# Up projections of a conv-gated MLP: two couples of groups per layer with tokens on the partitions, parking in later groups

## The chip, the cores and the metric

The kernel runs on one core of a Trainium2 chip, as one launch. The metric is the device time in microseconds, the median over the runs, with the lowest and highest of them. Besides, one execution was recorded by the hardware profiler; its rows are what "the trace" means here. All times are microseconds unless marked otherwise.

## The reference

A trunk of two layers works on x of 256 tokens by 2048, all in fp32. Each layer mixes tokens (layer 0 a spatial gating unit, layer 1 a latent attention), adds the residual, normalizes, and then runs a gated MLP with a causal convolution of width 3:

```python
def conv_ffn(x, w_up, conv_w, conv_b, w_down):
    h = x @ w_up                       # 256 x 2048 by 2048 x 11008
    h = lax.conv_general_dilated(h, conv_w[:, None, :], ...) + conv_b
    a, g = jnp.split(h, 2, axis=-1)
    return (jax.nn.silu(g) * a) @ w_down

x = layer_norm(ALPHA * x + m, ln_mix_g[i], ln_mix_b[i])
f = conv_ffn(x, ffn_w_up[i], ffn_conv_w[i], ffn_conv_b[i], ffn_w_down[i])
x = layer_norm(ALPHA * x + f, ln_ffn_g[i], ln_ffn_b[i])
```

The change concerns `h = x @ w_up` of both layers.

## The kernel before, in words

**Numbers in two parts.** TensorE multiplies fp32r parts. Every fp32 weight is split into a high part, a cast on ScalarE (`_cast`, L127), and a low part, the rest, a subtraction on VectorE (L130); activations are split likewise (`xhl`: 256 columns high and 256 low). A product takes high by high, high by low and low by high.

**The feed.** `Feed` holds one list of weight chunks of 1 MB (128 x 2048) in the order of use. `next()` gives the next chunk's parts and keeps loads (SP's queue, `_load`) and splits (`_split`) some chunks ahead. The parts lie in slots of the "big" pool, so a split waits until TensorE is through with the chunk that held its slot before. A chunk has a kind. A plain one ("") is split in two halves of 1024 columns. A "wide" one is split whole. A "seven" one (`_seven`) holds a 2 x 2 arrangement of four 512-column blocks; besides high and low parts of three blocks, VectorE builds sums of blocks (`ts`, L137) which are split as well (`th`, `tl`), so that seven block products do the work of eight. The other factor has to be summed in the same way (`xs`, split into high and low in `combine`).

**Two ways round.** In `prod_a` the weights stand still and the tokens move: four accumulators per group, each a 128-feature block by 512 columns (tokens by the high part, tokens by the low part); a plain chunk takes 16 matmuls of 512 columns (high weights by both parts) and 16 of 256 (low weights by the high part). `sum_halves` adds the two halves when the group is done (a copy of the low half on ScalarE, L388, and an add on VectorE into `h`, L390). In `prod_b` the activations stand still and 512 columns of weights move; tokens lie on the partitions, and a wide chunk takes 24 matmuls of 512 columns, a seven chunk 21. The V and U stages, at the kernel's begin, and the down projections run that way, with the class `Banks`: `eight` for wide chunks, `seven` for seven chunks, `rest` for the four VectorE additions that make the results out of the seven products. Four accumulators (`DIRECT`: q3, p2, e, q4) take the direct sums and four (`OWN`: p1, q5, p7, p6) the own products: all eight PSUM banks.

**The up projection.** Per layer 86 plain chunks: group 0 is done at the boundary to the norm (`upf`), groups 1 to 20 have four chunks each and group 21 has two. A group gives two pairs (a block of `a` and the fitting block of `g`). `pair` runs each through the convolution (`conv`: a ScalarE step L994, two VectorE steps L995 and L997, twice), SiLU (L1011) and the product into `act` (L1012). The eight banks hold two groups, so a group's pairs are worked off while the next group's matmuls run.

**Beside it.** The down projection will use eight chunks per layer whose seven-sums are prepared ahead during the up projection, "parked": `park` loads a chunk on GpSimd's queue (`praw`), splits and sums it (L154, L168, L169) and stores the parts to DRAM; `fetch` brings them back later. It is cut into steps, and each `next(jobs)` in the group loop does one: load, first split and store, sums, second split and store. Before, two steps stand in each group from 2 on (the second and third chunk), until the eight chunks are through. Also in this loop the norm's residual is multiplied and shifted (`old.restore`, groups 2 to 5) and put away in DRAM (`old.park`, groups 4 and 6).

The order of the instructions on each engine is set by a scheduler from the program's order and dependencies, except for the parts pinned into program order (parking, and some of TensorE's).

Of the kernel before, what the change touches and what calls it, by code (L numbers as in the profile page):

```python
# [8 lines left out]
F32 = mybir.dt.float32  # L9
F32R = mybir.dt.float32r  # L10
# [58 lines left out]
FIRST = ((19, 1), (20, 0), (20, 2))  # L69
LEAD = 5  # L70
KEEP = {"wide": 4, "seven": 6, "parked": 6}


def plan(n_k):
# [137 lines left out]
def trunk(ctx: ExitStack, tc: tile.TileContext, x, xT, gm_in, gm_wout, ffn_up, ffn_dn,  # L212
# [12 lines left out]
    def slot(shape, name, dt=F32, tag="big"):  # L225
        return big.tile(shape, dt, tag=tag, name=name, bufs=SLOTS[tag])
# [30 lines left out]
    def back(w, n_k):  # L257

        for hf, units in enumerate(plan(n_k)):
            c = slice(hf * 1024, (hf + 1) * 1024)  # L260
            for u, kind in units:
                if 2 * u + 1 == n_k:
                    chunks.append((w[2 * u, :, c], 1024, kind))
                    continue
                if kind == "parked":
                    parked.append(len(chunks))
                chunks.append((w[2 * u : 2 * u + 2, :, c].rearrange("k p c -> p k c"), 2048, kind))

    back(gm_wout, NF_GM)
    chunks += [(ffn_up[0, i], 2048, "") for i in range(n_up)]  # L270
    back(ffn_dn[0], NF_FF)
    chunks += [(ml_q[i], 2048, "") for i in range(4)]
    chunks += [(ml_kv[i], 3 * KVR, "") for i in range(5)] + [(ml_kv[5, :, 0:KVR], KVR, "")]
    chunks += [(ml_b[i], 2048, "") for i in range(ml_b.shape[0])]
    chunks += [(ml_out[i], 2048, "seven" if i - ml_out.shape[0] // 2 in MO_SEVEN else "") for i in range(ml_out.shape[0])]
    chunks += [(ffn_up[1, i], 2048, "") for i in range(n_up)]
    back(ffn_dn[1], NF_FF)


# [18 lines left out]
    def combine(name, o, k1, k2):  # L298


        t = tp.tile([P, 4, P], F32, tag="t2", name=f"xs{name}", bufs=T2)
        turn(t, k1, k2)
        o = o.rearrange("p (h s c) -> p h s c", h=2, s=4)
        nc.scalar.copy(o[:, 0], t)
        nc.vector.tensor_tensor(o[:, 1], t, o[:, 0].bitcast(F32), ALU.subtract)
        return [(o[:, 0, i], o[:, 1, i]) for i in (1, 2, 0, 3)]
# [221 lines left out]
    def down(n_k, src, tag, ln, acts, skew=SKEW, tiles=None, beside=None):  # L528

        ln.begin()  # L530
        seq = plan(n_k)
        line = seq[0] + seq[1]
        late, at = [], 0
        fetched = max([i for i, t in enumerate(line) if t[1] == "parked"], default=len(line))

        def again(v2, p):

            if src is not pT or p >= len(seq[0]) or v2 in line[p + 1 : p + 1 + KEEP[v2[1]]]:
                return None
            kind2 = dict(seq[1])[v2[0]]  # L540
            return "wide" if kind2 != v2[1] else kind2

        for hf, units in enumerate(seq):
            n = len(units)
            last = [u for u, kind in units if kind != "wide"][-1]
            acc = nxt if hf else Banks(f"{tag}{hf}", DIRECT + OWN, tiles)
            for i, (u, kind) in enumerate(units):
                left = n - 1 - i if hf == 1 else n
                if src is pT and at >= n - 3:
                    for v2 in line[at + 3 : at + 5]:  # L550
                        acts.bring(*v2)
                for n2, v2 in enumerate(line[at : at + 3]):
                    acts.make(*v2, again=again(v2, at + n2), tag="side" if at + n2 > fetched or at + n2 >= len(seq[0]) and v2[1] == "parked" and v2[0] < 20 else "big")
                if i == n - 8 and hf == 0:
                    ln.fetch(0)
                if i == n - 6 and hf == 0:
                    ln.fetch(1, "big" if src is pT else "side")
                if i == n - 2 and hf == 0:
                    nxt = Banks(f"{tag}1", OWN + DIRECT, seeded=True)
                    ln.seed(1, nxt)  # L560
                got = feed.next(splits=2 if left > 5 or left == 0 else 3, loads=2 if left > 2 or left == 0 else 1)
                if left == 6:
                    ln.prep()
                if left == 2 and ln.last:
                    ln.halves()
                if beside and at == 2:
                    beside()
                a, sums = acts.got[u]
                if left < skew:
                    late.append((a, *got))  # L570
                elif kind == "wide":
                    acc.eight(a, *got)
                else:
                    acc.seven(a, sums, *got, 512 if kind == "parked" else 0)
                    if u == last and hf:
                        parts = acc.rest(ln.room(hf))
                        if ln.last:
                            ln.whole(1, 3, acc.acc["q4"], parts[3])
                    elif u == last:
                        for j, t in enumerate(acc.rest()):  # L580
                            ln.fold(j // 2, 2 * hf + j % 2, t)
                at += 1
                for v2 in [v2 for v2 in acts.got if not any(v2 == w2 and n2 < KEEP[kind2]
                                                            for n2, (w2, kind2) in enumerate(line[at:]))]:
                    acts.got.pop(v2)
            if hf == 0:
                for j, m in enumerate(DIRECT):
                    ln.piece(j // 2, j % 2, acc.acc[m])

        def end(b, f):  # L590
            for i, (a, hi, lo) in enumerate(late):
                for j in range(len(a[b])):
                    prod_b([acc.acc[DIRECT[2 * b + f - 2]]], a[b][j], hi, lo, [(j * 1024 + (f - 2) * 512, 512)],
                           False, i == len(late) - 1 and j == len(a[b]) - 1)

        return [[None, None] + [acc.acc[DIRECT[2 * b + f]] for f in range(2)] for b in range(2)], end
# [404 lines left out]
    def ffn(layer, ln, acc, end, last):  # L1001
        act = [None] * 6
        acts = Acts(act, f"dn{layer}", NF_FF)

        def pair(a, acc_a, acc_g):
            if act[a // 8] is None:
                act[a // 8] = slot([P, 8, S], f"act{layer}_{a // 8}", tag="side" if a // 8 > 3 else "big")
            ca = conv(layer, a, acc_a, f"{layer}a{a}")
            cg = conv(layer, NF_FF + a, acc_g, f"{layer}g{a}")
            s = tp.tile([P, S], F32, tag="t1", name=f"s{layer}_{a}", bufs=T1)  # L1010
            nc.scalar.activation(s, cg, AF.Silu)  # L1011
            nc.vector.tensor_tensor(act[a // 8][:, a % 8, :], s, ca, ALU.mult)  # L1012

        hb, ht = [], [None, None]

        def after(b, step, acc):
            if step == 0:
                ht[b] = tp.tile([P, 512], F32, tag="t2", name=f"upt{layer}_{b}", bufs=T2)
                nc.scalar.copy(ht[b], acc)
                return  # L1020
            if b == 0:
                hb.extend(bank(f"uph{layer}_{f}") for f in range(2))
            for f in range(4):
                o = (f % 2) * S + b * P
                nc.tensor.transpose(hb[f // 2][:, o : o + P], ht[b][:, f * P : (f + 1) * P], ident)

        boundary(ln, acc, end, f"upf{layer}_", after)
        xhl, old = ln.new, ln
        jobs = park_all(feed.used + 2 * n_up)
        for gi in range(1, 22):  # L1030
            nt, nk = (4, 4) if gi < 21 else (2, 8)
            acc = [bank(f"up{layer}_{gi}_{f}") for f in range(nt)]
            for c in range(KD // nk):
                hi, lo = feed.next()
                prod_a(acc, xhl, range(nk * c, nk * c + nk), hi, lo)
                if gi > 1 and c in (1, 2) and gi + c > 3:
                    next(jobs, None)
                if (gi, c) in FIRST:
                    acts.make(*plan(NF_FF)[0][FIRST.index((gi, c))])
                if gi == 1 and c == 0:  # L1040
                    after(1, 1, None)
                    for f in range(2):
                        pair(f, hb[0][:, f * S : (f + 1) * S], hb[1][:, f * S : (f + 1) * S])
            for f in range(nt // 2):
                pair(2 * gi + f, acc[f], acc[nt // 2 + f])
            if 1 < gi < 6:
                old.restore(gi - 2)
            if gi in (4, 6):
                old.park(gi // 2 - 2)
        ln = Norm(2 * layer + 1, {}, old.put_away, last)  # L1050
        return (ln, *down(NF_FF, act, f"dn{layer}", ln, acts, 4 if last else SKEW))

# [429 lines left out]
```

## Time and profile before

| | |
|---|---|
| median of 3 runs | 2457.16 (2456.21 to 2458.2) |
| the profiled execution | 2456.78 |
| its span in the trace | 2454.6 |
| granted TensorE clock | 1.00 |
| GpSimd (POOL) busy | 140.3 |
| HBM read, written | 552.35 MB, 72.93 MB |

The page of the profile gives the busy time of each engine, the chain of work that ended last, the costliest groups of instructions and the transfers. A row of the timeline has start, duration, engine, line of the kernel, operation, what it writes and reads, shape and count. Durations of neighbours on one engine overlap; what an instruction costs in a queue is the distance from its start to the next start. PE is TensorE's matmuls, PEld its weight loads, DVE VectorE, ACT ScalarE, POOL GpSimd, SP SyncE.

### The profile page before, as it was taken

To read this page: it belongs to the slowest core of one execution; us is meant where nothing else is said; L and a number is where in the kernel's file an instruction comes from. 1 tells how busy PE (TensorE), PEld (TensorE's weight loads), DVE (VectorE), ACT (ScalarE), POOL (GpSimd) and SP (SyncE) were. 2 spreads that over 40 slices of the span, in tenths; PEclk is the share of its full clock that TensorE was granted. 3 is DMA by queue.
4 is the path that set the end of the run, shared out by engine and by line. 5 is a ranking of instruction groups with operands and counts; after the bars stand their busy time and mean duration, and the time that the engine had idled before them with its cause. 6 is when DMAs were issued, how large, how long until landed. Compare 5 with 4: busy or idle time off the path is not lost.

```text
span 2454.6 us, 32596 instructions
## 1 busy us (share of the span) xinstructions
PE 2447.1 (100%) x12394; PEld 2081.1 (85%) x12394; DVE 2099.4 (86%) x2813; ACT 1491.8 (61%) x2015; POOL 140.3 (6%) x261
## 2 busy tenths in 40 slices
PE   9999999999999999999999999999999999999999
PEld 7888888888888888888888888988888888888887
DVE  7999999889998788787779897878788787878998
ACT  6666665566576566556555566665665665656554
POOL 0000000001010000000000000000000000000000
PEclk9999999999999999999999999999999999999999
DMA  7555666659797778778868885544578787867895
GB/s 292 203 206 206 230 202 205 206 175 305 251 297 253 248 281 331 271 291 296 329 215 321 318 297 170 189 146 145 211 263 314 274 312 294 300 265 265 314 340 193
DMA packets 124668, 627.40 MB, mean 256 GB/s; under 512 B 11592, under 2 KB 15184, under 8 KB 83424
## 3 DMA queue, kind: packets, MB, share of 16 engines
q1 hardware_dynamic: 90128, 462.47, 53.2%
q0 software_dynamic: 34384, 162.86, 17.8%
q8 instruction: 97, 1.59, 0.3%
q14 instruction: 59, 0.48, 0.1%
HBM read 552.35 MB, written 72.93 MB: 255 GB/s over the span
## 4 chain that ended last, share of the span: by engine, by line
PE 97%; DVE 1%; DMA 1%; ACT 0%; issue 0%; SPq 0%; ACTq 0%; DVEq 0%
PE up L232 37%; PE ub L232 16%; PE dn_q L232 8%; PE dn_p L232 6%; PE v_q L232 5%; PE v_p L232 4%; PE wo_q L232 2%; PE dn_e L232 2%; PE wo_p L232 2%; PE upf L232 2%; PE mo L232 2%; PE v_e L232 2%; PE mkv L232 1%; PE qn L232 1%; PE mq L232 1%; PE kn L232 1%
## 5 line engine op out<-in xcount | busy, mean ns | idle before, releaser
L130 DVE TENSOR_TENSOR wl<-raw,wh 128x1024 fp32r<-128x1024 f32 (+4 forms) x643 | 950.9, 1493 | 145.0 <-ACT wh L127 112.9
L127 ACT CAST wh<-raw 128x1024 fp32r<-128x1024 f32 (+4 forms) x643 | 803.9, 1272 | 339.3 <-PE up L232 85.6
L232 PE MATMUL up<-xhl,wh 128*128 128x512 f32 x2624 | 611.3, 390 | 0.0
L232 PEld LDWEIGHTS up<-xhl,wh 128*128 128x128 f32 x2624 | 487.3, 188 | 97.8
L232 PEld LDWEIGHTS up<-xhl,wl 128*128 128x128 f32 x2624 | 325.8, 192 | 6.4
L232 PE MATMUL up<-xhl,wl 128*128 128x256 f32 x2624 | 328.1, 283 | 0.0
L127 ACT CAST th<-ts 128x1536 fp32r<-128x1536 f32 (+1 forms) x162 | 168.0, 1051 | 138.6 <-DVE ts L137 119.3
L130 DVE TENSOR_TENSOR tl<-ts,th 128x1536 fp32r<-128x1536 f32 (+1 forms) x162 | 191.1, 1217 | 6.4 <-PE v_p L232 1.9
L232 PE MATMUL ub<-wh,xhl 128*128 128x512 f32 x564 | 175.7, 393 | 0.0
L232 PEld LDWEIGHTS ub<-wh,xhl 128*128 128x128 f32 x564 | 105.9, 188 | 23.7 <-issue 1.9
L137 DVE TENSOR_TENSOR ts<-ts,raw 128x512 f32<-128x512 f32 x162 | 111.0, 685 | 1.6
L232 PE MATMUL ub<-wl,xhl 128*128 128x512 f32 x282 | 109.8, 389 | 0.0
L137 DVE TENSOR_TENSOR ts<-raw 128x1024 f32<-128x1024 f32 x81 | 98.6, 1217 | 2.3 <-DMA raw<-in_gm_in_dram 1.0
L232 PE MATMUL v_q<-wh,xhl 128*128 128x512 f32 x224 | 70.7, 391 | 0.8 <-ACT wh L127 0.8
L232 PEld LDWEIGHTS ub<-wl,xhl 128*128 128x128 f32 x282 | 52.9, 188 | 11.1
L232 PE MATMUL v_p<-wh,xhl 128*128 128x512 f32 x192 | 60.0, 389 | 0.0
L232 PEld LDWEIGHTS v_q<-wh,xhl 128*128 128x128 f32 x224 | 42.0, 188 | 10.3 <-ACT wh L127 1.6
L811 ACT ACTIVATE lny<-lnt,lncol 128x128 f32<-128x128 f32 x96 | 36.7, 472 | 15.3 <-PE lnt L807 15.2
L154 DVE TENSOR_TENSOR praw<-praw 128x512 f32<-128x512 f32 x64 | 43.9, 685 | 0.6
L390 DVE TENSOR_TENSOR h_1a<-up,lo_1a 128x256 f32<-128x256 f32 x41 | 17.2, 419 | 31.2 <-ACT lo_1a L388 31.2
L390 DVE TENSOR_TENSOR h_0a<-up,lo_0a 128x256 f32<-128x256 f32 x41 | 17.2, 419 | 31.0 <-ACT lo_0a L388 31.0
L232 PE MATMUL v_q<-wl,xhl 128*128 128x512 f32 x112 | 43.6, 389 | 0.0
(1992 smaller groups left out, 4442.1 us busy)
## 6 DMA issues: line engine op xcount, KB each, us to landing
raw<-in_ffn_up_dram SPq DMA_DIRECT2D x172, 1024.0 KB, 7.2
raw<-in_gm_in_dram SPq DMA_DIRECT2D x93, 1024.0 KB, 5.2
raw<-in_ffn_dn_dram SPq DMA_DIRECT2D x68, 1024.0 KB, 6.9
raw<-in_gm_wout_dram SPq DMA_DIRECT2D x48, 1024.0 KB, 6.6
praw<-in_ffn_dn_dram POOLq DMA_DIRECT2D x16, 1024.0 KB, 15.2
keptth<-pth POOLq DMA_DIRECT2D x16, 1024.0 KB, 8.8
kepttl<-ptl POOLq DMA_DIRECT2D x16, 1024.0 KB, 9.5
fth<-keptth POOLq DMA_DIRECT2D x16, 1024.0 KB, 10.4
```

What stands on the lines that cost most here:

```text
L127: cast = self.nc.scalar.copy(hi, raw)
L130: self.nc.vector.tensor_tensor(lo, raw, hi.bitcast(F32), ALU.subtract)
L137: add = lambda o, a, b: self.nc.vector.tensor_tensor(o, a, b, ALU.add)
L154: add = lambda o, a, b: pin(nc.vector.tensor_tensor(o, a, b, ALU.add))
L232: recent[0] = nc.tensor.matmul(o, l, r, start=start, stop=stop, skip_group_check=True)
L390: nc.vector.tensor_tensor(h, acc[:, 0:S], lo, ALU.add)
L811: nc.scalar.activation(y[:, j], t[:, j * P : (j + 1) * P], AF.Identity, bias=lncol[:, o : o + 1], scale=lncol[:, g : g + 1])
```

## The change

In each layer groups 5 and 6, and groups 8 and 9, become couples. A couple's eight chunks are cut anew: each takes one half (1024 columns) of the chunk of the same place in either group, so that it holds two steps of 128 along the 2048 inputs by the 512 features of each group, a 2 x 2 arrangement of blocks. They run with tokens on the partitions (`prod_b`, `Banks`, all eight banks) in the order `UP_PAIRS`; four of the eight are seven chunks. The activation sums for these are made in groups 2 to 4 by `combine_up`, four per layer. When the couple is done, `rest` and four adds give four tiles of 128 tokens by 512 features. After the first chunk of the plain group that follows, 16 transposes (`turn_back`) bring them back to features on the partitions, into four banks, and their four pairs are done after that group's second and third chunk, with no `sum_halves`.

Restoring and putting away the residual go to groups 1 to 4 (`EARLY`). Parking goes to one step each in groups 4 and 7 and three steps per group from group 10 on. The act tiles 0 and 1 now lie in the "side" pool and 2 to 5 in "big" (before: 0 to 3 in big, 4 and 5 in side).

```diff
+UP = [(1,), (2,), (3,), (4,), (5, 6), (7,), (8, 9), *((i,) for i in range(10, 22))]
+UP_PAIRS = [0, 2, 1, 3, 5, 4, 6, 7]
+UP_SEVEN = (2, 3, 4, 6)
+EARLY = {(1, 2): ("restore", 0), (2, 1): ("combine", 0), (2, 2): ("restore", 1), (2, 3): ("park", 0),
+         (3, 1): ("restore", 2), (3, 2): ("combine", 1), (3, 3): ("restore", 3), (4, 0): ("park", 1),
+         (4, 1): ("combine", 2), (4, 2): ("combine", 3)}
...
+    def up(w):
+        for gis in ((0,), *UP):
+            if len(gis) == 1:
+                chunks.extend((w[i], 2048, "") for i in range(4 * gis[0], min(4 * gis[0] + 4, n_up)))
+                continue
+            for p in UP_PAIRS:
+                i = 4 * gis[0] + p // 2
+                t = w[i : i + 5 : 4, :, p % 2 * 1024 : p % 2 * 1024 + 1024].rearrange("f p c -> p f c")
+                chunks.append((t, 2048, "seven" if p in UP_SEVEN else "wide"))
...
-                act[a // 8] = slot([P, 8, S], f"act{layer}_{a // 8}", tag="side" if a // 8 > 3 else "big")
+                act[a // 8] = slot([P, 8, S], f"act{layer}_{a // 8}", tag="side" if a // 8 < 2 else "big")
...
+        def turn_back(t, src, b):
+            for f in range(4):
+                o = (f % 2) * S + b * P
+                nc.tensor.transpose(t[f // 2][:, o : o + P], src[:, f * P : (f + 1) * P], ident)
+
+        def both(gi, t):
+            for f in range(2):
+                pair(2 * gi + f, t[0][:, f * S : (f + 1) * S], t[1][:, f * S : (f + 1) * S])
...
+        def combine_up(p):
+            x = xhl[p // 2][:, p % 2 * 2 : p % 2 * 2 + 2]
+            y = tp.tile([P, 2, S], F32, tag="t2", name=f"upy{layer}_{p}", bufs=T2)
+            nc.vector.tensor_tensor(y, x[:, :, 0:S].bitcast(F32), x[:, :, S : 2 * S].bitcast(F32), ALU.add)
+            if len(sums) % 2 == 0:
+                rooms.append(slot([P, 2, 8 * P], f"xu{layer}_{p}", F32R))
+            sums[p] = combine(f"u{layer}_{p}", rooms[-1][:, len(sums) % 2, :], y[:, 0], y[:, 1])
...
-                if gi > 1 and c in (1, 2) and gi + c > 3:
+                if c == 0 and turned:
+                    for i, t in enumerate(turned[2]):
+                        turn_back(turned[1][i % 2], t, i // 2)
+                if turned and 0 < c < 3:
+                    both(turned[0][c - 1], turned[1][c - 1])
+                if (gi > 9 and c > 0) or (gi, c) in ((4, 3), (7, 3)):
                     next(jobs, None)
...
+        def summed(gis):
+            acc = Banks(f"up{layer}_{gis[0]}", DIRECT + OWN)
+            for p in UP_PAIRS:
+                a = [[x_parts(xhl, 2 * p + j, b) for j in range(2)] for b in range(2)]
+                got = feed.next()
+                if p in UP_SEVEN:
+                    acc.seven(a, sums[p], *got, turned=512, across=True)
+                    if p == UP_SEVEN[-1]:
+                        rest = acc.rest()
+                else:
+                    acc.eight(a, *got, across=True)
+            for n, t in zip(DIRECT, rest):
+                nc.vector.tensor_tensor(t, acc.acc[n], t, ALU.add)
+            return gis, [[bank(f"upr{layer}_{gi}_{f}") for f in range(2)] for gi in gis], rest
```

How the order moves is shown at the start of the first couple, where group 4's four accumulators (`up0_4_0` to `up0_4_3`) are still to be read. On TensorE before, group 5's first chunk, chunk 164, begins with the weights (`wh164`) at rest and the activations moving:

```order
L232 MATMUL up0_5_0_7051<-xhl1_0_5891,wh164_6920 128x512 [waits Activation_49]
L232 MATMUL up0_5_1_7052<-xhl1_0_5891,wh164_6920 128x512 [waits DVE_49]
L232 MATMUL up0_5_2_7053<-xhl1_0_5891,wh164_6920 128x512 [waits DVE_49]
L232 MATMUL up0_5_3_7054<-xhl1_0_5891,wh164_6920 128x512 [waits DVE_49,PE_49]
L232 MATMUL up0_5_0_7051<-xhl1_0_5891,wh164_6920 128x512
```

On TensorE now, the couple's second and third chunks (165, a seven chunk, and 166, a wide one; `q5`, `q3`, `p2`, `p7` are accumulators of the couple, and an own product such as `p7` takes a bank that group 4 has to leave):

```order
L239 MATMUL up0_5_q5_7088<-th165_6997,xu0_2_6488 128x512 [waits DVE_49]
L239 MATMUL up0_5_q5_7088<-th165_6997,xu0_2_6488 128x512
L239 MATMUL up0_5_q5_7088<-tl165_6998,xu0_2_6488 128x512
L239 MATMUL up0_5_q3_7083<-wh166_7091,xhl1_0_5891 128x512 x2
L239 MATMUL up0_5_q3_7083<-wl166_7092,xhl1_0_5891 128x512
L239 MATMUL up0_5_q3_7083<-wh166_7091,xhl1_0_5891 128x512 x2
L239 MATMUL up0_5_q3_7083<-wl166_7092,xhl1_0_5891 128x512
L239 MATMUL up0_5_p2_7084<-wh166_7091,xhl1_0_5891 128x512 x2
L239 MATMUL up0_5_p2_7084<-wl166_7092,xhl1_0_5891 128x512
L239 MATMUL up0_5_p2_7084<-wh166_7091,xhl1_0_5891 128x512
L239 MATMUL up0_5_p7_7089<-th165_6997,xu0_2_6488 128x512 [waits DVE_49]
L239 MATMUL up0_5_p7_7089<-th165_6997,xu0_2_6488 128x512
```

What moved: the scheduler has put ten matmuls of chunk 166 between `q5` and `p7` of chunk 165; `p6` follows after three more matmuls of 166. `q5` takes the bank of `up0_4_2`, `p7` that of `up0_4_1` and `p6` that of `up0_4_3`, which VectorE reads for `h_0g8`, `h_0a9` and `h_0g9`.

On VectorE before, the same pairs of group 4 (8 and 9) stand between plain splits:

```order
L390 TENSOR_TENSOR h_0a8_7005<-up0_4_0_6828,lo_0a8_7003 128x256 [waits Activation_49]
L995 SCALAR_TENSOR_TENSOR c_0a8_7007<-h_0a8_7005,cst_176,c_0a8_7007 128x255 [waits Activation_49]
L390 TENSOR_TENSOR h_0g8_7013<-up0_4_2_6830,lo_0g8_7011 128x256 [waits Activation_49]
L997 SCALAR_TENSOR_TENSOR c_0a8_7007<-h_0a8_7005,cst_176,c_0a8_7007 128x254 [waits DVE_49]
L995 SCALAR_TENSOR_TENSOR c_0g8_7015<-h_0g8_7013,cst_176,c_0g8_7015 128x255 [waits Activation_49]
L997 SCALAR_TENSOR_TENSOR c_0g8_7015<-h_0g8_7013,cst_176,c_0g8_7015 128x254 [waits DVE_49]
L1012 TENSOR_TENSOR act0_1_7002<-s0_8_7019,c_0a8_7007 128x256 [waits Activation_49]
L390 TENSOR_TENSOR h_0a9_7024<-up0_4_1_6829,lo_0a9_7022 128x256 [waits Activation_49]
```

On VectorE now, between `h_0g8` and `h_0a9`:

```order
L408 TENSOR_TENSOR h_0g8_7055<-up0_4_2_6853,lo_0g8_7053 128x256 [waits Activation_49]
L1015 SCALAR_TENSOR_TENSOR c_0a8_7049<-h_0a8_7047,cst_176,c_0a8_7049 128x254 [waits DVE_49]
L144 TENSOR_TENSOR ts167_7121<-raw167_7008 128x1024 [waits DMAHW2_49,PE_49]
L1013 SCALAR_TENSOR_TENSOR c_0g8_7057<-h_0g8_7055,cst_176,c_0g8_7057 128x255 [waits Activation_49]
L144 TENSOR_TENSOR ts167_7121<-ts167_7121,raw167_7008 128x512 [waits DVE_49]
L1015 SCALAR_TENSOR_TENSOR c_0g8_7057<-h_0g8_7055,cst_176,c_0g8_7057 128x254 [waits DVE_49]
L137 TENSOR_TENSOR wl167_7123<-raw167_7008,wh167_7122 128x1536 [waits PE_49,Activation_49]
L144 TENSOR_TENSOR ts167_7121<-ts167_7121,raw167_7008 128x512 [waits DVE_49]
L1030 TENSOR_TENSOR act0_1_7044<-s0_8_7061,c_0a8_7049 128x256 [waits Activation_49]
L408 TENSOR_TENSOR h_0a9_7066<-up0_4_1_6852,lo_0a9_7064 128x256 [waits Activation_49]
```

What moved: the seven chunk 167's sums and first split now stand ahead of `h_0a9`, and the first of them waits (`PE_49`) until TensorE has left a slot. Lines of the changed kernel lie a little further down: L239, L137, L144, L408, L1013, L1015 and L1030 are L232, L130, L137, L390, L995, L997 and L1012 of before.

More of the change, by code (lines that the diff above doesn't have):

```diff
@@ L267, in back @@
                 chunks.append((w[2 * u : 2 * u + 2, :, c].rearrange("k p c -> p k c"), 2048, kind))
+    def up(w):
[7 more added lines that the diff above has]
+                chunks.append((t, 2048, "seven" if p in UP_SEVEN else "wide"))
     back(gm_wout, NF_GM)
-    chunks += [(ffn_up[0, i], 2048, "") for i in range(n_up)]
+    up(ffn_up[0])
     back(ffn_dn[0], NF_FF)
@@ L275, in trunk @@
     chunks += [(ml_out[i], 2048, "seven" if i - ml_out.shape[0] // 2 in MO_SEVEN else "") for i in range(ml_out.shape[0])]
-    chunks += [(ffn_up[1, i], 2048, "") for i in range(n_up)]
+    up(ffn_up[1])
     back(ffn_dn[1], NF_FF)
@@ L552, in down @@
                 for n2, v2 in enumerate(line[at : at + 3]):
-                    acts.make(*v2, again=again(v2, at + n2), tag="side" if at + n2 > fetched or at + n2 >= len(seq[0]) and v2[1] == "parked" and v2[0] < 20 else "big")
+                    acts.make(*v2, again=again(v2, at + n2), tag="side" if at + n2 > fetched else "big")
                 if i == n - 8 and hf == 0:
@@ L1022, in after @@
                 hb.extend(bank(f"uph{layer}_{f}") for f in range(2))
-            for f in range(4):
-                o = (f % 2) * S + b * P
-                nc.tensor.transpose(hb[f // 2][:, o : o + P], ht[b][:, f * P : (f + 1) * P], ident)
+            turn_back(hb, ht[b], b)
         boundary(ln, acc, end, f"upf{layer}_", after)
@@ L1029, in ffn, with plain @@
         jobs = park_all(feed.used + 2 * n_up)
-        for gi in range(1, 22):
+        sums, rooms = {}, []
+        def combine_up(p):
[5 more added lines that the diff above has]
+            sums[p] = combine(f"u{layer}_{p}", rooms[-1][:, len(sums) % 2, :], y[:, 0], y[:, 1])
+        early = {"restore": old.restore, "park": old.park, "combine": lambda i: combine_up(UP_SEVEN[i])}
+        def plain(gi, turned):
             nt, nk = (4, 4) if gi < 21 else (2, 8)
@@ L1041, in ffn @@
                     after(1, 1, None)
-                    for f in range(2):
-                        pair(f, hb[0][:, f * S : (f + 1) * S], hb[1][:, f * S : (f + 1) * S])
+                    both(0, hb)
+                if (gi, c) in EARLY:
+                    name, i = EARLY[gi, c]
+                    early[name](i)
             for f in range(nt // 2):
                 pair(2 * gi + f, acc[f], acc[nt // 2 + f])
[L1046 to L1049, printed above, removed]
+        def summed(gis):
[12 more added lines that the diff above has]
+            return gis, [[bank(f"upr{layer}_{gi}_{f}") for f in range(2)] for gi in gis], rest
+        turned = None
+        for gis in UP:
+            if len(gis) == 2:
+                turned = summed(gis)
+            else:
+                plain(gis[0], turned)
+                turned = None
         ln = Norm(2 * layer + 1, {}, old.put_away, last)
```

## The prediction

> **What bounds the kernel now.** I read the page first (busy times, then the chain), then what TensorE waited for, then its rows in the two kinds of place that the change makes alike.
>
> ```profile
> PE 2447.1 (100%) x12394; PEld 2081.1 (85%) x12394; DVE 2099.4 (86%) x2813; ACT 1491.8 (61%) x2015; POOL 140.3 (6%) x261
> PE 97%; DVE 1%; DMA 1%; ACT 0%; issue 0%; SPq 0%; ACTq 0%; DVEq 0%
> ```
>
> The next rows are TensorE's waits in the whole run: what it waited for, us in total, times, longest.
>
> ```profile
> PE warm L232 <- POOL idle L283: 1.3, 1, 1.3
> PE v_q L232 <- ACT wh L127: 0.8, 1, 0.8
> PE fin L232 <- DVE dg L788: 0.6, 1, 0.6
> PE pt L1276 <- DVE p L1268: 0.2, 1, 0.2
> ```
>
> They sum to 2.9 us of the span of 2454.6. TensorE is the bound in every stage, so a matmul taken away is worth its full time, as long as no other engine or transfer comes late in its place. The busiest of the others is VectorE (86%), and the change gives it more to do. The profiled execution took 2456.78, which is 2.2 above its span and 0.4 below the median of the runs, 2457.16. I make the sum against 2456.78 and move it by that 0.4.
>
> **The matmuls.** First a plain chunk pair in the stage (start, duration, matmuls), and the first row of the next pair:
>
> ```profile
> 907.93 7.44 PE L232 MATMUL up<-xhl,wh 128*128 128x512 f32 x32
> 915.21 4.00 PE L232 MATMUL up<-xhl,wl 128*128 128x256 f32 x32
> 919.05 1.32 PE L232 MATMUL up<-xhl,wh 128*128 128x512 f32 x5
> ```
>
> From start to start, 32 matmuls of 512 columns take 7.28 and 32 of 256 take 3.84. That is 11.12 for two chunks, 5.56 a chunk; eight of them in a row are the second window below (44.46). Now the first matmuls of a seven chunk of the V stage, of the wide chunk behind it and of the next seven chunk:
>
> ```profile
> 96.78 0.62 PE L232 MATMUL v_q<-wh,xc 128*128 128x512 f32 x2
> ...
> 101.53 0.62 PE L232 MATMUL v_q<-wh,xhl 128*128 128x512 f32 x2
> ...
> 106.97 0.62 PE L232 MATMUL v_q<-wh,xc 128*128 128x512 f32 x2
> ```
>
> The seven chunk takes 4.75 (21 matmuls) and the wide one 5.44 (24 matmuls), 0.2265 a matmul. The first window here is four wide and four seven chunks in the order that a couple has; the second is the eight plain chunks:
>
> ```profile
> 91.33:132.13 40.80, 40.80 (x181) 33.78 (x180) 39.60 (x37) 27.28 (x33) 0.00 (x0) 1.00 0.57 206
> 907.93:952.39 44.46, 44.46 (x259) 39.37 (x258) 39.27 (x50) 30.02 (x39) 3.97 (x7) 1.00 0.91 335
> ```
>
> Columns: length, then the busy time of PE, PEld, DVE, ACT, POOL, the granted clock (1.00 in both), DMA share, GB/s. A couple replaces eight plain chunks by the same mix as the first window. The gain is 44.46 - 40.80 = 3.66 a couple, **14.6 for the four**.
>
> **The way back.** Behind each couple stand 16 transposes of 128x128 in one run, 64 in the kernel. The before kernel has such a run elsewhere; I quote it with the two rows behind it, and the span of durations of one:
>
> ```profile
> 361.26 1.91 PE L945 MATMUL ub<-ident,v 128*128 128x128 f32 x16
> 362.92 0.71 PE L232 MATMUL ub<-wh,xc 128*128 128x512 f32 x2
> 363.47 0.39 PE L232 MATMUL ub<-wl,xc 128*128 128x512 f32 x1
> L945 PE MATMUL ub<-ident,v x96: 270/273/273, 314.5 to 546.3; 128*128 128x128 f32 x96
> ```
>
> The next matmul starts 1.66 after the first transpose, and the two matmuls behind it take 0.55 where two take 0.45 at 0.2265 each: 1.66 + 0.10, about 1.75 a run, 0.104 a transpose. **Four runs cost 7.0.** The bounds: by columns alone, a quarter of a 512-column matmul, 64 x 0.057 = 3.6; by their own duration with nothing overlapped, 64 x 0.273 = 17.5. I take the row, since it is the same instruction in the same number. [...]
>
> **VectorE.** Its instructions are priced from start to start, in two places, the plain stage and the V stage:
>
> ```profile
> 907.27 0.42 DVE L390 TENSOR_TENSOR h_0g<-up,lo_0g 128x256 f32<-128x256 f32 x1
> 907.61 0.47 DVE L997 SCALAR_TENSOR_TENSOR c_0a<-h_0a,cst,c_0a 128x254 f32<-128x254 f32 x1
> 908.00 1.22 DVE L130 TENSOR_TENSOR wl<-raw,wh 128x1024 fp32r<-128x1024 f32 x1
> 909.13 0.47 DVE L995 SCALAR_TENSOR_TENSOR c_0g<-h_0g,cst,c_0g 128x255 f32<-128x255 f32 x1
> ...
> 913.86 0.42 DVE L1012 TENSOR_TENSOR act<-s,c_0a 128x256 f32<-128x256 f32 x1
> 914.20 2.35 DVE L130 TENSOR_TENSOR wl<-raw,wh 128x1024 fp32r<-128x1024 f32 x2
> ```
>
> ```profile
> 91.72 1.75 DVE L130 TENSOR_TENSOR tl<-ts,th 128x1536 fp32r<-128x1536 f32 x1
> 93.39 0.68 DVE L875 TENSOR_TENSOR v<-v_q,v1w 128x512 f32<-128x512 f32 x1
> 93.99 0.68 DVE L875 TENSOR_TENSOR v<-v_p,v1p 128x512 f32<-128x512 f32 x1
> ...
> 96.39 2.28 DVE L130 TENSOR_TENSOR wl<-raw,wh 128x2048 fp32r<-128x2048 f32 x1
> 98.59 1.22 DVE L137 TENSOR_TENSOR ts<-raw 128x1024 f32<-128x1024 f32 x1
> ```
>
> So h 0.34, a conv step 0.39, act 0.34, 1024 columns 1.13, 1536 1.67, 512 0.60, 2048 2.20. A seven chunk's split (1024 + 3 x 512 + 2 x 1536) takes 6.27, a wide one 2.20. A couple has 4 x 6.27 + 4 x 2.20 + 8 x 0.60 (its `rest` and the four adds) = 38.7, and on top the two pairs of the group ahead, 2 x (2 x 0.34 + 4 x 0.39 + 0.34) = 5.2. That is 43.9 in TensorE's 40.8: VectorE falls behind by 3.1 within a couple. The plain group behind it has 4 x 2 x 1.13 for the splits and 4 x 1.90 for the couple's pairs (no h), 16.7 of its 24.0 (22.2 + 1.75), so the arrears go there, if the lookahead of the weights holds 3.1. The V window is my evidence that such a mix runs at all: 39.60 busy of 40.80 and no wait of TensorE.
>
> Where it is tight is the start of a couple. With T its start: the sum `ts167` needs the slot that chunk 164's high part leaves at T + 5.44. From there stand, in the order shown above, 1024 + 2 x 512 + 1536 columns, two conv steps, an act and `h_0a9`: 1.13 + 1.20 + 1.67 + 0.78 + 0.34 + 0.34 = 5.46, so bank `up0_4_1` is free at about T + 11.0 with 0.1 of signalling. TensorE reaches `p7`, which takes that bank, after 24 + 15 + 10 matmuls, T + 11.1. `p6` needs `h_0g9`, one conv step, its ScalarE step and an h later, against 55 matmuls, T + 12.5:
>
> ```profile
> 905.60 0.60 ACT L994 ACTIVATE c_0a<-h_0a,cst 128x256 f32<-128x256 f32 x1
> ```
>
> That chain, 0.60 + 0.47 + 0.42 and hand-overs, gives about T + 12.7. So I see 0.2 late at each of the two banks, less than the error of such a sum. The stall is between 0 and 0.75 a couple; I take 0.3, **1.2 for four**. Behind a late `p7` stands all of TensorE's queue, since it runs in order; VectorE itself waits for nobody there.
>
> **Parking and restoring.** Before carries two parking steps a group, after three in groups 10 to 20:
>
> ```profile
> raw<-in_ffn_up_dram SPq DMA_DIRECT2D x172, 1024.0 KB, 7.2
> praw<-in_ffn_dn_dram POOLq DMA_DIRECT2D x16, 1024.0 KB, 15.2
> ```
>
> A chunk parked moves 1 MB in and 3.5 MB out, four steps, so three quarters of it per group: 4 + 3.4 pieces of 1.05 MB in 22.2 us is near 348 GB/s. The second window above carried 335 with no wait of TensorE; the 13 more are part of the parking rival. In VectorE a group has 9.0 + 5.2 + 0.75 x 6.3 = 18.9 of 22.2. I price this at nothing, the cover being ScalarE's lead on TensorE:
>
> ```profile
>   DMA raw<-in_ffn_up_dram: 59.2, 24
> ```
>
> Those are idle times before instructions on the weights' landing buffers, 24 waits for a transfer, 59.2 us in all, and none reached TensorE. Restoring the residual is 16 adds and products of 512 columns, 9.6 us of VectorE a layer, and only moves; the four activation sums are new, 8 instructions of 512 columns and 12 of 128, at most 8 x 0.60 + 12 x 0.39 = 9.5 a layer. Both lie in groups 1 to 4, where a plain group leaves VectorE 22.2 - 14.2 = 8.0 and parking has gone; nothing as well, and a few us a layer if that room doesn't hold. SP's queue keeps its one load a chunk; the couple's two-piece form is the one that the u stage loads.
>
> **Sum.** 2456.78 - 14.6 + 7.0 + 1.2 = 2450.4, and 0.4 more for the median: **2450.8**. With stalls of 0 to 3 it is 2449.6 to 2452.6.
>
> **The rivals.**
> - *VectorE bounds the couples.* For: 43.9 against 40.8. If none of the 3.1 is carried over, 12.4 stand in place of my 1.2: 2462.0. If its instructions cost their durations (1.22, 0.68, 1.75, 2.28, 0.42, 0.47), a couple has 47.9, 7.1 too much, 28.4 in four: 2478.0. Against: starts lie 0.08 nearer than durations in every row above, and the V window. [...] Chance 0.20, most of it below 2462.
> - *Parking bounds the late groups: the slower side.* With three steps a group, two of the eight parked chunks of a layer have only two chunks' time (11.1) from load to first cast, against a landing of 15.2. The cast would hold ScalarE 4.1 us, and the weight casts stand behind it: four times 4.1 is 16.4, **2467.2**. It decides if ScalarE's lead is below 4.1 there. Against: of the 24 waits none got through. Chance 0.10.
> - *Transposes not overlapped*, 17.5 instead of 7.0: 2461.3. Chance 0.05.
> - *The saving isn't there*: the couples run at the plain pace, because weights or buffers come no faster than before. Without the 14.6 it is 2465.4. Against: the V stage needs the same 206 GB/s. Chance 0.05.
>
> **How the numbers follow.** My forecast has 0.60. About 0.2% of the time, 4.9 us, is what a measurement of this kernel can tell from no change, so faster means below 2452.2 and slower above 2462.1. Of the forecast's 0.60, 0.57 lie below 2452.2. Same takes the 0.03 left, 0.15 of VectorE's case and the transposes' 0.05: 0.23. Slower has 0.05 of VectorE's, 0.10 and 0.05: 0.20. The range begins half way to the transposes by columns (2446.2), at 2448.0, and ends at 2464.0, past VectorE's 12.4; above it lie parts of three cases, under 0.2.
>
> **What would show it.** Right: a couple takes 41 us, its seven chunks 4.75; each of the four runs of transposes moves the next matmul by 1.75; TensorE waits for `h_0a9`'s and `h_0g9`'s lines at the start of a couple for under 1 us; VectorE's busy time rises by 80 to 95 us (by durations 16 x (6.76 - 2.44) + 32 x 0.68 - 32 x 0.42 = 77, and the sums). Wrong: waits of TensorE for the low parts of a couple's late chunks (VectorE), or for high parts in groups 10 to 20 with ScalarE idle on `praw` (parking), or a run of transposes of 4 us.

## The result, and the profile after

The changed kernel takes 2538.95 us in the median of 5 runs (2538.0 to 2543.95), against 2457.16 before: 1.0338 times as long, 95% interval 1.0323 to 1.0353. I had forecast 2450.8. The profiled execution took 2543.95, the longest of the five, and its span is 2542.2.

The busy times of the changed kernel:

```profile
PE 2474.6 (97%) x12154; PEld 2085.3 (82%) x12154; DVE 2183.1 (86%) x2909; ACT 1509.0 (59%) x1995; POOL 140.3 (6%) x261
```

TensorE has 240 matmuls fewer and yet is 27.5 us longer busy, and idle for 67.6 of the span where it was idle for 7.5. What it waited for in the changed kernel (us in total, times, longest):

```profile
PE up L239 <- DVE h_0g L408: 17.3, 5, 5.5
PE up L239 <- DVE h_1g L408: 16.2, 5, 5.5
PE up L239 <- DVE wl L137: 12.6, 7, 3.3
PE up L239 <- ACT wh L134: 9.2, 4, 3.5
...
```

With two more lines, 2.6 for `h_0a` and 1.5 for `h_1a`, these are 59.4 us. All lie in plain groups from 10 on, none in a couple. Before, there were none of them. The lines name VectorE's `h` and `wl`, but VectorE is late there itself. The idle times before instructions on the parked chunk's landing tile `praw`, first of the kernel before, then of the changed one:

```profile
  DMA praw<-in_ffn_dn_dram: 4.8, 3
```

```profile
  DMA praw<-in_ffn_dn_dram: 112.8, 14
```

ScalarE stood still for 112.8 us at 14 of the 16 first casts (`pwh`) of a parked chunk, 8.1 each, waiting for the chunk's load. One of them, with what follows on each engine. GpSimd's queue (the chunk before stores its second parts, then the load is issued):

```profile
1137.13 0.53 POOL L166 DMA_DIRECT2D keptth<-pth  x1 [9.45 <-ACT pth L175]
1140.74 0.53 POOL L166 DMA_DIRECT2D kepttl<-ptl  x1 [3.09 <-DVE ptl L176]
1141.28 0.71 POOL L171 DMA_DIRECT2D praw<-in_ffn_dn_dram  x1
```

ScalarE, from the second part's cast of the chunk before to the late cast:

```profile
1134.93 1.91 ACT L175 CAST pth<-praw 128x2048 fp32r<-128x2048 f32 x1
...
1155.47 1.48 ACT L175 CAST pwh<-praw 128x1536 fp32r<-128x1536 f32 x1 [8.52 <-DMA praw<-in_ffn_dn_dram]
```

VectorE, which has the low part of the same tile in its queue, and TensorE:

```profile
1156.98 1.76 DVE L176 TENSOR_TENSOR pwl<-praw,pwh 128x1536 fp32r<-128x1536 f32 x1 [8.68 <-ACT pwh L175]
```

```profile
1162.52 0.49 PE L239 MATMUL up<-xhl,wh 128*128 128x512 f32 x1 [2.19 <-DVE h_0a L408]
1165.80 5.62 PE L239 MATMUL up<-xhl,wh 128*128 128x512 f32 x13 [2.79 <-DVE h_0g L408]
```

This is one chain. The load stands in GpSimd's queue behind the store `kepttl`, which waited 3.09 for VectorE's `ptl`, and is issued 0.54 after it: 6.35 after the cast `pth` began (1134.93 to 1141.28). It lands some 14 later. ScalarE has come to the next first cast at 1146.95, 12.0 after `pth`, and waits 8.52 with everything behind it: the weight casts and the copies `lo` that free the accumulators. In all 14 late chunks the load is issued 4.9 to 13.1 before its cast is due and takes 12.9 to 19.3 to land. VectorE waits as long at `pwl`, `h` comes late, and the next group's matmuls find their bank still occupied.

Most of the rest of the loss is the clock. Windows of 2 us of the changed kernel around a wait of 5.48 (length, busy time of PE, PEld, DVE, ACT, POOL, granted clock, DMA share, GB/s):

```profile
1190.00:1192.00 2.00, 0.70 (x4) 0.23 (x2) 0.00 (x0) 0.00 (x0) 0.00 (x0) 1.00 0.07 27
...
1194.00:1196.00 2.00, 0.00 (x0) 0.00 (x0) 2.00 (x4) 2.00 (x4) 0.76 (x2) 0.72 0.57 240
1196.00:1198.00 2.00, 1.82 (x4) 1.49 (x5) 2.00 (x4) 0.67 (x2) 0.14 (x1) 0.50 0.90 366
1198.00:1200.00 2.00, 2.00 (x6) 1.59 (x5) 2.00 (x4) 0.00 (x0) 0.00 (x0) 0.50 0.72 214
1200.00:1202.00 2.00, 2.00 (x7) 1.58 (x7) 1.97 (x5) 0.68 (x2) 0.00 (x0) 0.57 0.85 332
1202.00:1204.00 2.00, 2.00 (x19) 2.00 (x18) 1.33 (x4) 0.86 (x2) 0.00 (x0) 1.00 0.41 168
```

TensorE stops near 1190.7, the clock falls to a half at 1194.9, and is back at 1.00 only near 1201.7, 5.5 after work has begun again at 1196.2. In between, matmuls of 512 columns start 0.427 apart (eleven steps from 1196.74 to 1201.44) and not 0.2265. There are twelve such stretches, all within the late groups of the two layers, 68.3 us long in all, and TensorE is busy for 53.9 of them. Over the whole run the mean granted clock is 0.986, against 1.00 before.

### The profile page after: what moved, and what is told of

Same layout as the page of the kernel before. It is cut to its first block, busy times and chain, and to the rows that moved or that the text cites. A ratio compares the mean times of both kernels' runs of the same rounds, so it can differ in the third digit from the quotient of the medians.

```text
span 2542.2 us, 32266 instructions
## 1 busy us (share of the span) xinstructions
PE 2474.6 (97%) x12154; PEld 2085.3 (82%) x12154; DVE 2183.1 (86%) x2909; ACT 1509.0 (59%) x1995; POOL 140.3 (6%) x261
## 4 chain that ended last, share of the span: by engine, by line
PE 65%; issue 28%; DMA 3%; DVE 2%; POOL 1%; ACT 1%; POOLq 0%; SPq 0%; DVEq 0%; ACTq 0%
PE ub L239 16%; PE dn_q L239 8%; PE dn_p L239 7%; PE up L239 5%; PE v_q L239 5%; PE v_p L239 4%; PE dn_e L239 2%; DMA praw<-in_ffn_dn_dram 2%; PE wo_q L239 2%; PE wo_p L239 2%; PE upf L239 2%; PE mo L239 2%; PE v_e L239 2%; PE mkv L239 1%; PE qn L239 1%
## 5 line engine op out<-in xcount | busy, mean ns | idle before, releaser
L137 DVE TENSOR_TENSOR wl<-raw,wh 128x1024 fp32r<-128x1024 f32 (+5 forms) x611 | 935.7, 1550 | 105.6 <-ACT wh L134 87.8
L134 ACT CAST wh<-raw 128x1024 fp32r<-128x1024 f32 (+5 forms) x611 | 790.2, 1317 | 268.8 <-DMA raw<-in_ffn_up_dram 64.3
L239 PE MATMUL up<-xhl,wh 128*128 128x512 f32 x2112 | 520.9, 404 | 46.9 <-DVE h_0g L408 17.3
L239 PEld LDWEIGHTS up<-xhl,wh 128*128 128x128 f32 x2112 | 407.6, 196 | 137.7 <-issue 36.9
L134 ACT CAST th<-ts 128x1536 fp32r<-128x1536 f32 x194 | 201.3, 1052 | 169.0 <-DVE ts L144 148.5
L239 PE MATMUL up<-xhl,wl 128*128 128x256 f32 x2112 | 269.5, 285 | 12.6 <-DVE wl L137 12.6
L239 PEld LDWEIGHTS up<-xhl,wl 128*128 128x128 f32 x2112 | 265.3, 193 | 19.6 <-DVE wl L137 14.2
L137 DVE TENSOR_TENSOR tl<-ts,th 128x1536 fp32r<-128x1536 f32 x194 | 229.2, 1218 | 8.5 <-ACT th L134 3.6
L239 PE MATMUL ub<-wh,xhl 128*128 128x512 f32 x564 | 175.7, 393 | 0.0
L144 DVE TENSOR_TENSOR ts<-ts,raw 128x512 f32<-128x512 f32 x194 | 133.1, 686 | 1.9
L176 DVE TENSOR_TENSOR pwl<-praw,pwh 128x1536 fp32r<-128x1536 f32 x16 | 28.1, 1757 | 122.4 <-ACT pwh L175 122.4
L239 PEld LDWEIGHTS ub<-wh,xhl 128*128 128x128 f32 x564 | 105.9, 188 | 23.7 <-issue 1.9
L144 DVE TENSOR_TENSOR ts<-raw 128x1024 f32<-128x1024 f32 x97 | 118.2, 1218 | 3.9 <-DMA raw<-in_ffn_up_dram 1.4
L239 PE MATMUL ub<-wl,xhl 128*128 128x512 f32 x282 | 109.8, 389 | 0.0
L175 ACT CAST pwh<-praw 128x1536 fp32r<-128x1536 f32 x16 | 23.6, 1477 | 112.8 <-DMA praw<-in_ffn_dn_dram 112.8
L239 PE MATMUL v_q<-wh,xhl 128*128 128x512 f32 x224 | 71.4, 394 | 0.5 <-ACT wh L134 0.5
L239 PEld LDWEIGHTS ub<-wl,xhl 128*128 128x128 f32 x282 | 52.9, 188 | 11.1
L239 PE MATMUL v_p<-wh,xhl 128*128 128x512 f32 x192 | 60.4, 391 | 0.0
L239 PEld LDWEIGHTS v_q<-wh,xhl 128*128 128x128 f32 x224 | 42.5, 190 | 10.3 <-ACT wh L134 1.5
L239 PE MATMUL v_q<-wl,xhl 128*128 128x512 f32 x112 | 43.8, 391 | 0.0
```

Source lines behind the costliest of these rows:

```text
L134: cast = self.nc.scalar.copy(hi, raw)
L137: self.nc.vector.tensor_tensor(lo, raw, hi.bitcast(F32), ALU.subtract)
L144: add = lambda o, a, b: self.nc.vector.tensor_tensor(o, a, b, ALU.add)
L175: pin(nc.scalar.copy(hi[:, 0:cols], raw[:, o : o + cols]))
L176: pin(nc.vector.tensor_tensor(lo[:, 0:cols], raw[:, o : o + cols], hi[:, 0:cols].bitcast(F32), ALU.subtract))
L239: recent[0] = nc.tensor.matmul(o, l, r, start=start, stop=stop, skip_group_check=True)
```

## The experiments

**The load ahead of the stores.** Only the place of the load in GpSimd's queue is changed: the next chunk's load is issued in the step of the second part, ahead of its two stores.

```diff
-        raw = tile("praw", F32)
-        pin(nc.gpsimd.dma_start(raw.rearrange("p (k c) -> p k c", k=ap.shape[1]), ap))
+        raw = self.praw.pop(i) if i in self.praw else self.bring(i)
         yield
...
                 add(r[3], r[3], r[2])
                 yield
+                if nxt is not None:
+                    self.praw[nxt] = self.bring(nxt)
```

> The changed kernel with one thing moved: the load of the next parked chunk stands in GpSimd's queue ahead of the two second-part stores of the chunk before, not behind them; every step of the parking stays at its place otherwise. Theory (the load is issued too late, behind stores that wait for VectorE, so that the cast of the next chunk blocks ScalarE): the cast's 112.8 us of waits fall below 20, TensorE's waits of 59 us in the late groups fall below 10, the granted clock returns to 1.00, and the time comes to 2450, 2445 to 2460. Rival (groups 10 to 20 move more bytes than the transfers can bring): the waits stay and the time is above 2510.

Measured: 2449.15 (2448.74 to 2449.22), 0.9968 of before, interval 0.9956 to 0.9981, clock 1.00. GpSimd's queue in this kernel, the load and behind it the first of the second part's stores:

```profile
1125.07 0.71 POOL L161 DMA_DIRECT2D praw<-in_ffn_dn_dram  x1
1136.26 0.56 POOL L173 DMA_DIRECT2D keptth<-pth  x1 [10.48 <-ACT pth L180]
```

```profile
1148.56 1.48 ACT L180 CAST pwh<-praw 128x1536 fp32r<-128x1536 f32 x1
```

The load leaves at 1125.07, 11.2 ahead of the first of the stores behind which it stood, and the cast at 1148.56 waits for nothing. No cast of this run waits for a load. Eight of the loads wait in GpSimd's queue, 23.9 us in all, until an earlier `kepttl` store has landed, and TensorE doesn't feel it: its waits are 2.6 us in the whole run, none in the up projections.

The steps, the bytes and the tiles are those of the changed kernel, so the bandwidth of the late groups is not the cause. By the medians the place of the load is worth 89.8. The two profiled executions, with the same work on every engine, differ by 94.9 of span (2542.2 - 2447.3): TensorE's idle time is 60.5 less (67.6 against 7.1) and its busy time 34.4 less. The busy row:

```profile
PE 2440.2 (100%) x12154; PEld 2065.7 (84%) x12154; DVE 2184.3 (89%) x2909; ACT 1510.3 (62%) x1995; POOL 140.3 (6%) x261
```

Some 27 of the 34.4 are matmuls at half clock: half of the 53.9 that TensorE was busy in those stretches. The other 7 or so lie outside them. A matmul that starts after a wait is on record with about 0.5 (the row at 1162.52), where one in a run adds 0.23, and some 26 such starts would make them up; I did not test that. This is also the best version: it beats the kernel before by 7.8.

**The late parking alone.** The kernel before, with no couples, gets the changed kernel's parking groups, act tiles' pools and earlier restoring.

```diff
-                if gi > 1 and c in (1, 2) and gi + c > 3:
+                if (gi > 9 and c > 0) or (gi, c) in ((4, 3), (7, 3)):
                     next(jobs, None)
```

> The kernel before, no couples, with only the late parking (one step in groups 4 and 7, three per group from 10), the act tiles' pools and the earlier restoring. Theory (parking alone costs it): 2457 + 59 of waits + 35 of clock, near 2550, 2530 to 2560. Rival (the couples' arrears on VectorE are carried into the later groups): within 10 of 2457.

Measured: 2530.22 (2529.72 to 2537.84), ratio 1.0305, interval 1.029 to 1.032. ScalarE's waits in it, and the two largest of TensorE's:

```profile
  DMA praw<-in_ffn_dn_dram: 98.0, 14
```

```profile
PE up L234 <- DVE h_1g L392: 11.9, 5, 3.7
PE up L234 <- DVE h_0g L392: 10.9, 4, 5.4
```

So 73 of the loss come without any couple. That is the lower edge of what I expected: TensorE is 46 longer idle and 27 longer busy than before, where I had put in 59 and 35, and ScalarE's waits are fewer (98.0 against 112.8). This kernel has the new pools and the earlier restoring as well, but so has the kernel with the early load, which loses nothing; so it is the parking. The rival, arrears of the couples that are carried on, is out as the main cause. Some 16 more of the 89.8 come only where the couples stand too, and go with the early load; how the couples add to it was not followed.

**Parking left out.** Nothing is loaded, split or stored for the parking, and the down projection fetches rows of other weights in place of the parked parts. A first pair of kernels took two short pieces per row from the weights of the down projection:

```diff
+        self.kept[i] = {n: ap[:, :, 0 : 768 if n[0] == "w" else 1024] for n in ("wh", "wl", "th", "tl")}
+        yield
```

> The changed kernel with the parking left out: nothing is loaded, split or stored for it, and the down projection fetches raw weights in place of the parked parts. Theory: no waits of TensorE in groups 10 to 20, clock 1.00, and 7.6 below before_no_park. Rival (the couples are what costs): 2500 or more.

> The kernel before with the parking left out in the same way. Theory: the parking was hidden there, so within 5 of 2457; the distance from after_no_park is the couples' own worth, 7.6 by the sum in the prediction. A rival by which the couples give nothing: equal to after_no_park within 2.

Measured: 2472.34 (2467.36 to 2476.57) and 2461.49 (2459.31 to 2464.72), so the first is 10.9 above the second and not 7.6 below. These say little on the couples: TensorE waited in the down projection for the substitute fetches themselves, 3.3 us in the second and far more in the changed kernel's variant:

```profile
PE dn_q L215 <- DMA ftl<-in_ffn_dn_dram: 17.2, 6, 4.6
```

A second pair fetches whole rows of an up weight (`self.flat[:, 0:1536]` or `[:, 0:2048]`).

> The changed kernel with the parking left out, and the down projection fetching rows of 8 or 6 KB of another weight in place of the parked parts, so that the fetches have the form that they have with parking. Theory: no waits of TensorE above the 2.9 of the kernel before, and 7 to 8 below before_no_park2. Rival (the couples slow the kernel): above it.

> The kernel before with the parking left out in that way. Theory: 2457 within 3, since the parking was hidden there. Rival: it had a price, and the time is below 2452.

Measured: 2449.79 (2449.16 to 2451.65) and 2457.52 (2456.27 to 2459.7). Both are as expected: the parking was free in the kernel before, and the couples are worth 7.7.

**A longer time between second part and next first part.** The load stays behind the stores. The steps are dealt out over groups 10 to 20 so that four chunks of TensorE, 22.2 us, lie between the two.

```diff
+TIMES = [(4, 3), (7, 3)] + [divmod(40 + o, 4) for k in range(8) for o in (6 * k - 1, 6 * k, 6 * k + 1) if o >= 0]
...
             yield from feed.park(i)
-            yield
...
-                if (gi > 9 and c > 0) or (gi, c) in ((4, 3), (7, 3)):
+                if (gi, c) in TIMES:
```

> The changed kernel with the parking's steps dealt out anew over the same groups: the load of the next chunk in the same step as the second part of the chunk before, still behind its stores in GpSimd's queue, and the next first part four chunks of TensorE later (22.2 us), as in the kernel before, in place of two or three. Theory (what decides is the time from the second part to the next first cast, against the stores' wait plus a landing of 15): the cast's waits fall below 15 us in all, TensorE waits for nothing in the late groups, 2449.5, 2446 to 2456. Rival (standing behind the stores is itself what makes the load late, whatever the gap): waits above 50 us on ScalarE and a time above 2480.

Measured: 2488.52 (2486.43 to 2490.16), ratio 1.0126, interval 1.0111 to 1.0141. My expectation was missed, and the time is what the rival had.

```profile
  DMA praw<-in_ffn_dn_dram: 43.1, 8
```

Half the casts wait, 5.4 each. Two more, with 5.13 and 3.97, begin 0.07 after their load has landed, though the profile names no releaser; with them ten of 16 wait 52.2, which is the rival's figure too. So this run alone speaks for the rival, and only the next one decides. What I had wrong is the distance. The steps stand four chunks apart in the program, but in the late cases a cast is due only 14 to 19 us after the `pth` before it; `pth` had itself waited up to 2.8 for VectorE's sums, and the rest I did not follow. In one case `pth` began at 1057.59 and its store was issued at 1059.80, the next cast was due at 1075.8, and the load, issued at 1063.24, came at 1080.2. From `pth`'s start to the landing are 2.2 + 3.4 + 17.0 = 22.6.

The next kernel puts the sums into the first part's step and lets five chunks (27.8) pass:

```diff
+TIMES = [(4, 3), (7, 3)] + [divmod(40 + o, 4) for k in range(8) for o in (6 * k - 1, 6 * k) if o >= 0]
...
             if n == "w":
-                yield
                 r = [raw[:, 512 * i : 512 * (i + 1)] for i in range(4)]
```

> As spread, with the sums of a parked chunk in the same step as its first part, so that the second part comes one chunk of TensorE later and the next first part five chunks (27.8 us) after that; the load still stands behind the stores. Theory (from spread: the second part's cast, its store's turn and the landing take 1.9 + 3.0 + 16.4 = 21.3 us, and the time from second part to next first cast was 18 there): with 27.8 the first casts wait for no load, below 10 us in all, TensorE waits for nothing in the late groups, and the time is 2450, 2447 to 2458. Rival (a load behind its stores is late whatever the gap): above 2475.

Measured: 2464.01 (2460.53 to 2466.3), ratio 1.0023, interval 1.0013 to 1.0034.

```profile
  DMA praw<-in_ffn_dn_dram: 4.5, 3
```

The load is behind its stores, its casts hardly wait, and no `up` line is left among TensorE's waits. So it is the distance in time that decides, not the queue's order as such. The time is above my 2458 and below the rival's 2475: the parking now ends in the groups where the down projection's first activations are made, and the waits stand there, 11 us in six lines, of which the largest is

```profile
PE dn_q L239 <- DVE dn00wx L519: 3.6, 1, 3.6
```

I did not follow those further.

**What a gap costs in clock.** In the kernel before, TensorE is made to wait in the V stage for fills on GpSimd, by small matmuls that add zero. In the first version the scheduler put other matmuls between the two that enclose a gap.

```diff
+            if c == 2 and gi in GAPS:
+                mm(acc.acc["q4"][:, 0:64], ident, gap[:, 0:64], False, False)
+                for _ in range(GAPS[gi]):
+                    nc.gpsimd.memset(gap, 0.0)
+                mm(acc.acc["q4"][:, 0:64], ident, gap[:, 0:64], False, False)
```

> The kernel before with five gaps put into the V stage, where TensorE waits for 2, 4, 6, 8 and 10 fills of a tile on GpSimd (some 1 to 5 us), with 10 small matmuls that add zero. [...] Rival: each gap, however short, costs clock in proportion to its length.

Measured: 2460.89, one run, with 0.4 us of waits for the fills in all: no gaps, so it shows nothing on the clock. In the second version the later matmuls are ordered behind the gap (`order(recent[0], gapped[0])` for each).

> As clock_gaps, with the matmuls behind each gap ordered after it, so that TensorE has nothing to do in the gaps (fills of 0.53 us: 2, 4, 6, 8 and 10 of them, some 1.1, 2.1, 3.2, 4.2 and 5.3 us and signalling). [...] Rival: clock lost in proportion to the gap.

Measured: 2486.19, one run, clock 0.996. The gaps, in the rows of the second small matmuls:

```profile
67.62 0.43 PE L233 MATMUL v_q<-gap,ident 128*128 128x64 f32 x2 [1.29 <-POOL gap L867]
111.50 0.69 PE L233 MATMUL v_q<-gap,ident 128*128 128x64 f32 x2 [2.38 <-POOL gap L867]
158.06 0.43 PE L233 MATMUL v_q<-gap,ident 128*128 128x64 f32 x2 [3.55 <-POOL gap L867]
205.88 0.69 PE L233 MATMUL v_q<-gap,ident 128*128 128x64 f32 x2 [4.71 <-POOL gap L867]
255.32 0.69 PE L233 MATMUL v_q<-gap,ident 128*128 128x64 f32 x2 [5.87 <-POOL gap L867]
```

The granted clock around the second gap and the fourth, in windows:

```profile
111.00:112.00 1.00, 0.50 (x3) 0.50 (x3) 0.94 (x2) 0.00 (x0) 0.45 (x1) 0.67 0.65 270
112.00:113.00 1.00, 1.00 (x4) 0.81 (x5) 0.00 (x0) 0.00 (x0) 0.00 (x0) 0.50 1.05 442
113.00:114.00 1.00, 1.00 (x4) 0.81 (x3) 0.00 (x0) 0.00 (x0) 0.00 (x0) 0.50 0.57 229
114.00:115.00 1.00, 1.00 (x5) 0.76 (x4) 0.00 (x0) 0.00 (x0) 0.00 (x0) 0.62 0.00 0
```

```profile
203.00:204.00 1.00, 0.00 (x0) 0.00 (x0) 0.97 (x2) 0.00 (x0) 0.94 (x2) 0.75 0.69 279
204.00:210.00 6.00, 4.12 (x11) 3.35 (x12) 0.02 (x1) 0.00 (x0) 1.65 (x4) 0.50 0.25 105
210.00:211.00 1.00, 1.00 (x5) 0.79 (x4) 0.81 (x1) 0.48 (x1) 0.00 (x0) 0.84 0.09 16
```

The gap of 1.29 left the clock at 1.00. That of 2.38 brought 3.4 us at a half (111.34 to 114.75), which I had not expected of so short a gap, and so did that of 3.55 (159.12 to 162.54); those of 4.71 and 5.87 brought 6.8 (203.50 to 210.32 for the first), in part within the gap. The clock's loss does not go with the length of the gap, as the rival had it; it goes in pieces of some 3.4. So it does in the changed kernel, whose twelve stretches are five of 3.41, six of 6.83 and one of 10.24.

Nor does the length alone decide whether a piece is lost. Two gaps of the changed kernel:

```profile
2128.10 1.22 PE L239 MATMUL up<-xhl,wl 128*128 128x256 f32 x8 [3.07 <-DVE wl L137]
2136.21 4.80 PE L239 MATMUL up<-xhl,wh 128*128 128x512 f32 x13 [2.05 <-DVE h_1g L408]
```

After the 3.07 the clock stayed at 1.00; after the 2.05 it was at a half from 2136.96 to 2140.37. What differs is where they fall. In the changed kernel the starts of the twelve half-clock stretches lie whole multiples of 3.413 apart (1058.35, 1136.85, 1164.16 and 1194.88: 23, 8 and 9 of them), and in the run with the gaps so do its four (111.34, 159.12, 203.50 and 254.70: 14, 13 and 15). On the changed kernel's grid, with a line at 2126.72, the gap of 3.07 (2125.03 to 2128.10) is cut into 1.69 and 1.38, and the gap of 2.05 (2134.15 to 2136.21) lies within one piece. In the up projections of that trace, each of the eleven pieces at full clock in which TensorE was idle for 2.07 or more is followed by one at a half; of two with 1.74 and 1.75 one is, at 1239.25, and one is not, at 1130.02.

## Why the prediction was wrong

**What held.** *The matmuls and the way back* came out as summed. The couples are worth 7.7 and 7.8 in two pairs of kernels, where I had 14.6 - 7.0 = 7.6 without stalls; in the second pair TensorE's busy time makes 6.9 of it (2447.1 against 2440.2). The rows of the kernel with the early load, at the second couple's end and through its transposes:

```profile
1006.49 3.79 PE L246 MATMUL up<-xhl,wh 128*128 128x512 f32 x16
...
1012.04 0.60 PE L1046 MATMUL upr<-ident,up_8w 128*128 128x128 f32 x4
...
1013.70 2.15 PE L246 MATMUL up<-xhl,wl 128*128 128x256 f32 x16
1015.69 7.44 PE L246 MATMUL up<-xhl,wh 128*128 128x512 f32 x32
```

The 16 transposes take 1.66 from start to start, and the 16 small matmuls behind them 1.99 where they take 1.92 elsewhere: 1.73, against my 1.75. This couple takes 40.8, from 965.69 to 1006.49; the first one takes 41.3, and those of the other layer 41.1 and 40.8. *The stall at a couple's start* was priced at 0.3; the 0.5 and 0.3 of each layer's first couple are of that size, the second ones have none. The working there has a slip: it finds 0.2 late at each of two banks, but by its own figures the first is free at T + 11.0, before the 11.1 at which TensorE comes. *VectorE* does not bound the couples: TensorE waits for it in none of them, and its busy time rose by 84, where I had 80 to 95.

**What failed** is the step "Parking and restoring": "I price this at nothing, the cover being ScalarE's lead on TensorE". The price was 89.8 by the medians (94.9 in the profiled executions), and three things in that step were wrong.

First, the time from load to cast. I counted two of a layer's eight chunks with two chunks' time (11.1) and took the rest as safe. By the positions in the program, with one step after each of the second to fourth chunks of a group, three loads stand two chunks ahead of their first cast and four only one (5.6). Against the landing of 15.2 that is 3 x 4.1 + 4 x 9.6 = 50.7 a layer, 101 in two layers, near the 112.8 measured: the rival's four waits should have been 14. The step at which the program issues the load was not the right start either. A load is issued when its queue comes to it, and it stands behind two stores that wait for ScalarE's cast and VectorE's low part: from `pth`'s start to the landing pass 19.6 to 24.7 in the late chunks, and 19.1 to 23.2 in the kernel before. The kernel before already showed that this was at its limit. Its casts:

```profile
879.09 1.92 ACT L168 CAST pth<-praw 128x2048 fp32r<-128x2048 f32 x1
909.70 1.48 ACT L168 CAST pwh<-praw 128x1536 fp32r<-128x1536 f32 x1
926.60 1.91 ACT L168 CAST pth<-praw 128x2048 fp32r<-128x2048 f32 x1
946.93 1.48 ACT L168 CAST pwh<-praw 128x1536 fp32r<-128x1536 f32 x1 [1.17 <-DMA praw<-in_ffn_dn_dram]
```

With 30.6 between them the cast found its data, with 20.3 it waited 1.17. The three waits of 4.8 us in all stood in the view that I used. The new schedule cut the four chunks between second part and next first part to two or three, 11 to 17 us, and all but two of the 16 casts were late.

Second, the cover. I took it from ScalarE's waits for weights, of which none reached TensorE. Those are waits for the chunk that is to be cast anyway. A wait at `pwh` holds ScalarE and VectorE at once, and behind it stand the copies and `h` of the finished group, which free the accumulators. The lead in weights doesn't help there: 33.5 of the 59.4 us are waits for `h_0g` and `h_1g`. Nor did it hold where it should: 21.8 are waits for `wl` and `wh`.

Third, the price of a wait. The rival with the right mechanism, parking at the late groups, had 16.4 from four waits of 4.1 and a chance of 0.10. There were 14 waits of 8.1, and TensorE paid 59.4 of the 112.8 as idle time and some 27 again as matmuls at half clock. No term for the clock stood in the forecast or in any rival. The sign named for that rival, ScalarE idle on `praw`, came; TensorE's waits were for `h` and low parts more than for the high parts that I had named (9.2).

## What to carry to other kernels

When steps with a transfer are dealt closer together, count the steps between load and first use for every chunk of the cycle, and write down for each queue what the transfer stands behind: it starts when that is let go, not at the step in which the program issues it (the load above left 0.54 after a store that had waited 3.09). A few small waits in the profile of before (here three, 4.8 us in all) show that such a distance is at its limit, so look at them before shortening it. Where TensorE is the bound, a gap costs its length and can cost matmuls at half clock as well (gaps of 2.05 and 2.38 did, one of 1.29 did not): here some 27 us beside 59.

## What the hardware showed that I had not expected

A gap of 2.38 us between dense matmuls was enough to bring TensorE's granted clock to 0.50 for 3.4 us (one gap of one run), and in the changed kernel one of 2.05 was; one of 1.29 was not, nor one of 3.07 that fell across a line of the grid of 3.413; one of 4.71 brought 6.8. The grid is no more than what the starts of the half-clock stretches give in these two runs. How long TensorE has to be idle between two of its lines is not settled here: 2.07 or more was enough each time in the up projections of the changed kernel, and at some 1.75 the two cases differ.
